# Gated delta rule on one core: triangular inverse in blocks of 16 joined to 32, other numbers between the steps, final norm in column halves

## The chip, the cores and the metric

The kernel runs on one core of a Trainium2 chip. The metric is device time in microseconds (us). The kernel before took 1869.27 us as the median of 3 runs (1867.79 to 1872.93).

## What is computed

The kernel computes one decoder layer for a prompt of 1024 columns (tokens) and for 8 samples of 4 columns, with the same weights: a projection `w_in`, two branches on parts of it (a gated delta rule and an HGRN2 recurrence), their projections, a gate, `w_out`, an FFN with a short convolution, and a final RMSNorm. The change touches the triangular solve of the delta rule and the final norm. Of the reference this matters:

```python
# _gated_delta: chunks of CHUNK_A = 64, 4 heads, key and value width 128
lmat = jnp.where(strict, jnp.einsum('nbhid,nbhjd->nbhij', kb, k) * decay, 0.0)
a_mat = eye + lmat
T = lax.linalg.triangular_solve(a_mat, jnp.broadcast_to(eye, a_mat.shape), left_side=True, lower=True)
value = jnp.einsum('nbhij,nbhje->nbhie', T, v * beta[..., None])
...
# per chunk, in sequence
u = value_n - jnp.einsum('bhcd,bhde->bhce', kcd_n, S)
o = jnp.einsum('bhcd,bhde->bhce', qg_n, S) + jnp.einsum('bhij,bhje->bhie', attn_n, u)
S = S * jnp.exp(gl_n)[..., None, None] + jnp.einsum('bhcd,bhce->bhde', kg_n, u)
...
# _rmsnorm, used at the end on the prompt and on the samples
y = xf * lax.rsqrt(jnp.mean(xf * xf, axis=-1, keepdims=True) + EPS) * g.astype(jnp.float32)
```

## The kernel before

**Dense work.** All 1056 columns go through one dense projection after another. Each f32 operand is split into a high and a low part (`whi`, `wlo`, `hhi`, `hlo`), and `mm3` (L105 to L111) adds three products: L109, L110 and L111. A *dense block* is one step of `proj_cm`: 8 row tiles by 3 products, 24 matmuls of 128x352 into one PSUM buffer, then one eviction. PSUM has four buffers for dense blocks (`PSD`) and four for all other products (`PSM`). Weights come in pairs of column tiles (`load_w`): a DMA on SP to `wraw` (L96), a cast to `whi` on ACT (L83) and a subtraction to `wlo` on DVE (L84). A pair serves 6 dense blocks; two pairs are in flight.

**What sets the order.** The engines take their instructions in program order. The two recurrences are generators, and between their steps they yield a number n; `drive` hands it to `fill`, a queue of the dense blocks of `w_in` (132 blocks in all), which then puts n blocks into the order:

```python
def __call__(self, n):
    self.acc += n
    while self.acc >= 1.0 and self.q:
        self.acc -= 1.0
        self.step()
```

After every second step, `drive` also puts in one step of the samples' own generator. The phases are: norm and first projections; HGRN in four groups of 256 columns (`hgrn_group`); the delta rule in four groups (`gdn_group`); the store of the conv cache (L245 to L249); then the load of the branch outputs `oT_d`, whatever is left of `fill`, the split to `ohi` and `olo`, the branch projections, `w_out`, the FFN in 11 chunks, and in the last chunk of `down` the final norm (L1294 to L1298, with `norm`, L169 to L177).

**One delta group.** It holds 8 pairs of a 128-column tile and a head. Transposes of q, k, v (L689), the decay matrices (L710) and the products of k with k and q (L718) give `UA` (L719, DVE): for each pair the transposed strictly lower matrix beside the attention matrix. Then:

- four DMAs on SP put the 32x32 diagonal blocks into `dU` in DRAM (L725), four more load `Db` (L730), laid out with one block to a partition of 1024 elements;
- DVE negates `Db` (L739) and substitutes row by row: 31 steps of a product `Pt` (L744) and a sum into `X` (L746), with yields of 0.7 at rows 8, 16 and 24;
- four DMAs on SP store `X` to `dX` (L750), four load it back as `Yd` (L756), now with the rows of a block on the partitions; a yield of 3.5;
- DVE transposes `Yd` to `Xd` (L758), ACT copies `Yd` into `UA` (L762);
- PE joins blocks of 32 to 64 (L768, L776, L779) and 64 to 128 (L791 to L797) by small products, with evictions between them;
- the chunk steps follow (L812 to L830), then `head_post` (L580 to L600) with a yield of 2.2 and the transposes L597, and the store to `oT_d` (L848).

In `X`, partition 32b+j holds column j of the eight blocks number b of the pairs:

```python
for r in range(1, 32):
    w = r + 1
    nc.vector.tensor_tensor(Pt[:, :, 0:w], X[:, :, 0:w],
                            Db[:, 0:w, r:w].rearrange("p s o -> p o s").broadcast_to([P, 8, w]), ALU.mult)
    nc.vector.tensor_reduce(X[:, :, r], Pt[:, :, 0:w], axis=mybir.AxisListType.X, op=ALU.add)
```

## Time and profile before

| | before |
|---|---|
| median of 3 runs | 1869.27 us |
| profiled execution | 1866.14 us |
| span of its trace | 1864.4 us |
| PE busy | 1738.4 us, 93% |
| DVE busy | 927.8 us, 50% |
| ACT busy | 526.4 us, 28% |
| POOL busy | 187.5 us, 10% |
| mean granted TensorE clock | 0.965 |

The profile is of one execution, which took 1866.14 us by the same measure as the median; its trace spans 1864.4 us. An engine is busy while one of its instructions runs; PE can be busy at full clock (granted clock 1.0) or below it. A line such as L768 names the line of the kernel, then come the operation, `out<-in` by the program's names, and the tile's size.

### The profile page before, as it was taken

Reading aid. Unit: us, or ns where it says so; the run is one execution under the profiler, and the core shown is the slowest. Engines: PE = TensorE matmul, PEld = TensorE weight load, DVE = VectorE, ACT = ScalarE, POOL = GpSimd, SP = SyncE. Lnnn points to the kernel's source line nnn. Section 1 sums busy time; section 2 is a strip of 40 time slices with the busy share of each in tenths; the row PEclk is TensorE's granted clock in tenths of the full one; section 3 lists DMA queues with packets and bytes.
Section 4 is the critical chain, followed back from the end, with each engine's and each line's share of the span. In section 5 each row is a group of like instructions: output and inputs, shape, how many; then the busy total and the mean of one; then the engine's idle time right before and its main releaser. Section 6 shows DMA issues by size and latency. Waiting matters only on the chain.

```text
span 1864.4 us, 30256 instructions
## 1 busy us (share of the span) xinstructions
PE 1738.4 (93%) x12765; PEld 1644.4 (88%) x12765; DVE 927.8 (50%) x1585; ACT 526.4 (28%) x1140; POOL 187.5 (10%) x315
## 2 busy tenths in 40 slices
PE   7999999989989999904999999999999999999998
PEld 7999989989978889803999999899899899899896
DVE  5312356774635666453552463444444444444446
ACT  5433323434324252303110242122122122122122
POOL 2100223340102020100000010000000000000001
PEclk9999999999989999856999999999999999999999
DMA  6323243444443363123343211111111111111102
GB/s 204 104 91 114 86 126 131 121 140 140 122 120 94 98 174 120 55 62 135 107 133 95 80 46 46 46 36 56 46 37 55 46 38 53 46 39 52 46 26 106
DMA packets 198931, 161.81 MB, mean 87 GB/s; under 512 B 17982, under 2 KB 184016, under 8 KB 198777
## 3 DMA queue, kind: packets, MB, share of 16 engines
q1 hardware_dynamic: 175382, 123.92, 22.6%
q10 hardware_dynamic: 23414, 35.96, 5.4%
q8 instruction: 100, 1.64, 0.4%
q14 instruction: 35, 0.29, 0.1%
HBM read 119.57 MB, written 40.21 MB: 86 GB/s over the span
## 4 chain that ended last, share of the span: by engine, by line
PE 53%; DVE 5%; ACT 2%; DMA 1%; issue 1%; POOL 1%; SPq 0%; ACTq 0%; POOLq 0%; DVEq 0%
PE pd L109 16%; PE pd L110 16%; PE pd L111 16%; DVE Pt L744 1%; DVE X L746 1%; PE pd L121 1%; POOL rs L76 1%; DVE y L177 1%; DVE tmp L177 0%; DMA raw<-oT_d 0%; PE pd L120 0%; ACT tmp L174 0%; PE pm L812 0%; DVE mlo L84 0%; PE pd L123 0%
## 5 line engine op out<-in xcount | busy, mean ns | idle before, releaser
L109 PE MATMUL pd<-hhi,whi 128*128 128x352 f32 x1056 | 351.3, 333 | 0.0
L110 PE MATMUL pd<-hlo,whi 128*128 128x352 f32 x1056 | 346.5, 328 | 0.0
L111 PE MATMUL pd<-hhi,wlo 128*128 128x352 f32 x1056 | 346.2, 328 | 0.0
L109 PE MATMUL pd<-mhi,whi 128*128 128x352 f32 x1056 | 340.5, 323 | 0.0
L110 PE MATMUL pd<-mlo,whi 128*128 128x352 f32 x1056 | 338.6, 321 | 0.6 <-DVE mlo L84 0.6
L111 PE MATMUL pd<-mhi,wlo 128*128 128x352 f32 x1056 | 338.4, 321 | 0.0
L84 DVE TENSOR_TENSOR wlo<-wraw,whi 128x1024 fp32r<-128x1024 f32 x126 | 153.3, 1227 | 198.0 <-ACT whi L83 197.5
L83 ACT CAST whi<-wraw 128x1024 fp32r<-128x1024 f32 x126 | 130.5, 1049 | 399.1 <-PE pd L111 201.9
L109 PEld LDWEIGHTS pd<-hhi,whi 128*128 128x128 f32 x1056 | 201.1, 190 | 2.2 <-issue 0.8
L110 PEld LDWEIGHTS pd<-hlo,whi 128*128 128x128 f32 x1056 | 201.4, 191 | 1.3 <-issue 0.4
L111 PEld LDWEIGHTS pd<-hhi,wlo 128*128 128x128 f32 x1056 | 201.0, 190 | 1.3 <-issue 0.6
L110 PEld LDWEIGHTS pd<-mlo,whi 128*128 128x128 f32 x1056 | 198.4, 188 | 1.3 <-DVE mlo L84 0.9
L109 PEld LDWEIGHTS pd<-mhi,whi 128*128 128x128 f32 x1056 | 198.1, 188 | 0.4
L111 PEld LDWEIGHTS pd<-mhi,wlo 128*128 128x128 f32 x1056 | 198.1, 188 | 0.0
L1289 DVE TENSOR_TENSOR x<-x,pd 128x512 f32<-128x512 f32 x176 | 118.8, 685 | 78.0 <-PE pd L111 77.6
L109 PE MATMUL pd<-whi,act 128*128 128x512 f32 x352 | 137.9, 392 | 0.1
L110 PE MATMUL pd<-wlo,act 128*128 128x512 f32 x352 | 137.2, 390 | 0.0
L111 PE MATMUL pd<-whi,act 128*128 128x512 f32 x352 | 137.0, 389 | 0.0
L218 ACT COPY z<-pd 128x352 f32<-128x352 f32 (+1 forms) x102 | 44.3, 441 | 143.7 <-PE pd L111 136.5
L1266 DVE TENSOR_TENSOR ga<-pd,ga 128x352 f32<-128x352 f32 x66 | 34.5, 522 | 98.3 <-PE pd L111 98.3
L109 PEld LDWEIGHTS pd<-whi,act 128*128 128x128 f32 x352 | 66.1, 188 | 16.2 <-PE pd L111 2.0
L109 PE MATMUL pd<-ohi,whi 128*128 128x352 f32 x192 | 62.6, 327 | 18.0 <-ACT ohi L83 18.0
(407 smaller groups left out, 2687.7 us busy)
## 6 DMA issues: line engine op xcount, KB each, us to landing
wraw<-in_w_in SPq DMA_DIRECT2D x48, 512.0 KB, 5.4
wraw<-in_w_ffn_gate SPq DMA_DIRECT2D x22, 512.0 KB, 5.0
wraw<-in_w_ffn_up SPq DMA_DIRECT2D x22, 512.0 KB, 3.7
wraw<-in_w_ffn_down SPq DMA_DIRECT2D x22, 512.0 KB, 4.0
sg_d<-sg ACTq DMA_DIRECT2D x16, 528.0 KB, 2.6
qkv_d<-sl ACTq DMA_DIRECT2D x12, 512.0 KB, 3.1
sga<-sg_d SPq DMA_DIRECT2D x12, 352.0 KB, 4.3
sgb<-sg_d SPq DMA_DIRECT2D x12, 352.0 KB, 3.0
```

The source lines that it names most:

```text
L76: nc.gpsimd.tensor_tensor(out, in_, pexp[:n, which, :w], ALU.pow)
L83: nc.scalar.copy(out=hi, in_=src)
L84: (eng or nc.vector).tensor_tensor(lo, src, hi.bitcast(F32), ALU.subtract)
L109: nc.tensor.matmul(ps, whi[:, kw], xhi[:, kx], start=q == 0, stop=False)
L110: nc.tensor.matmul(ps, whi[:, kw], xlo[:, kx], start=False, stop=False)
L111: nc.tensor.matmul(ps, wlo[:, kw], xhi[:, kx], start=False, stop=q == n - 1)
L121: nc.tensor.matmul(ps[:NS], st[:, kx, 0:NS], wlo[:, kw], start=False, stop=False)
L177: nc.vector.scalar_tensor_tensor(xn[:n], xt[:n], rs[:n], g_bc[:n], ALU.mult, ALU.mult)
L218: nc.scalar.copy(out=z[:, pad + a:pad + e], in_=ps[:, :e - a])
L744: nc.vector.tensor_tensor(Pt[:, :, 0:w], X[:, :, 0:w], Db[:, 0:w, r:w].rearrange("p s o -> p o s").broadcast_to([P, 8, w]), ALU.mult)
L1266: nc.vector.tensor_tensor(a[:, bs], ps, a[:, bs], ALU.mult)
L1289: nc.vector.tensor_tensor(x1[:, t, qs], x1[:, t, qs], ps, ALU.add)
```

## The change

The substitution runs on diagonal blocks of 16 instead of 32. Two blocks of 16 are joined to one of 32 on PE: 32 products of 32x16 from `UA` and `Xd` (L773), an eviction with the sign turned to `W5` (L774), 32 products of 32x16 from `W5` and `Yd` (L781), an addition into `Yd` (L782), a second transpose to `Xd` (L783). The old join of 32 to 64 follows as it was (L788, L794 and on). `dU` and `Yd` go in eight DMAs each of half the size, issued by SP and ACT in turn; `Db`, `X` and `Pt` shrink, and they have tiles of their own in place of shared ones. The numbers yielded fall: in a delta group 2.2 to 0.6 at the start of group 0, three yields of 0.7 in the substitution to one, 3.5 to 2.4 ahead of the transpose; two yields of 0.5 are new; `head_post` yields 2.0 for 2.2, an HGRN level 0.75 for 0.9. The 132 blocks stay 132: what isn't put between the steps comes after them. The final norm takes the squares of each half of 512 columns apart (`final_sq`), each as soon as the half is there, and multiplies and stores in halves (`final_out`), one row tile later.

```diff
-        yield 2.2
+        yield 2.0
...
-        yield 0.6 if g else 2.2
+        yield 0.6
...
         for b in range(4):
-            nc.sync.dma_start(out=dU[g, b:32:4].rearrange("c j i -> j c i"),
-                              in_=UA[32 * b:32 * b + 32, :, 0, 32 * b:32 * b + 32])
-
-        Db = os_tile([P, 32, 32], "Db")
+            for k in range(2):
+                r0 = 32 * b + 16 * k
+                (nc.sync, nc.scalar)[k].dma_start(out=dU[g, k, b:32:4].rearrange("c j i -> j c i"),
+                                                  in_=UA[r0:r0 + 16, :, 0, r0:r0 + 16])
+
+        Db = mp.tile([P, 16, 16], F32, name="Db", bufs=1)
         for b in range(4):
-            nc.sync.dma_start(out=Db[32 * b:32 * b + 32], in_=dU[g])
+            nc.sync.dma_start(out=Db[32 * b:32 * b + 32], in_=dU[g, b // 2])
...
+        nc.gpsimd.memset(Yd, 0.0)
...
-        for r in range(1, 32):
+        for r in range(1, 16):
...
         for b in range(4):
             nc.sync.dma_start(out=dX[g, :, 8 * b:8 * b + 8, :], in_=X[32 * b:32 * b + 32])
...
         for b in range(4):
-            nc.sync.dma_start(out=Yd[32 * b:32 * b + 32], in_=dX[g, b:32:4].rearrange("c s r -> s c r"))
-        yield 3.5
+            for k in range(2):
+                r0 = 32 * b + 16 * k
+                (nc.sync, nc.scalar)[k].dma_start(out=Yd[r0:r0 + 16, :, 16 * k:16 * k + 16],
+                                                  in_=dX[g, b:32:4, 16 * k:16 * k + 16].rearrange("c s r -> s c r"))
+        nc.gpsimd.memset(W5[:, :, 16:32], 0.0)
+        yield 2.4
+
         nc.vector.transpose(Xd, Yd)
+        pw = PSM()
+        pwv = pw[:, :128].rearrange("p (c s) -> p c s", s=16)
+        for p in range(8):
+            for b in range(4):
+                bs = slice(32 * b, 32 * b + 32)
+                nc.tensor.matmul(pwv[bs, p, :], UA[bs, p, 0, bs], Xd[bs, p, 0:16], start=True, stop=True)
+        nc.vector.tensor_scalar(W5[:, :, 0:16], pwv, -1.0, None, op0=ALU.mult)
+        yield 0.5
...
+                nc.tensor.matmul(pxv[bs, p, :], W5[bs, p, :], Yd[bs, p, 16:32], start=True, stop=True)
+        nc.vector.tensor_tensor(Yd[:, :, 16:32], pxv, Yd[:, :, 16:32], ALU.add)
+        nc.vector.transpose(Xd, Yd)
+        yield 0.5
...
-            yield 0.9
+            yield 0.75
...
+                if ch == NCH - 1:
+                    final_sq(t, q)
+                    if q == 0 and t != NC:
+                        final_out(t - 1 if t else NC)
...
+    def final_sq(t, q):
...
+        nc.scalar.activation(last["sq"][:n, t % NC, qs], x1t(t)[:n, qs], AF.Square, scale=D ** -0.5,
+                             accum_out=fsum[t][:n, q:q + 1])
...
+        nc.vector.scalar_tensor_tensor(rs[:n], ss[:n, 0:1], EPS, ss[:n, 1:2], ALU.add, ALU.add)
+        power(rs[:n], rs[:n], 0)
...
+        for q in range(2):
+            qs = slice(q * 512, (q + 1) * 512)
+            nc.vector.scalar_tensor_tensor(yt[:n, qs], x1t(t)[:n, qs], rs[:n], last["g"][:n, qs], ALU.mult, ALU.mult)
+            (nc.sync, nc.scalar)[q].dma_start(out=dst[:, qs], in_=yt[:n, qs])
```

What that makes of the order is shown at three places. First PE in the last delta group, from its last `L718` (`x_7752` is that group's q and k) to the first join of `Xd`; L109, L110 and L111 are the dense matmuls. Before:

```order
L718 MATMUL pm<-x_7752 128x256 x3
L710 MATMUL pm<-eem,A 128x128 x2
L109 MATMUL pd<-hhi,whi 128x352
L110 MATMUL pd<-hlo,whi 128x352
L111 MATMUL pd<-hhi,wlo 128x352
L718 MATMUL pm<-x_7752 128x256
L768 MATMUL pm<-Xd,UA 32x32 x16
```

Now, at the joins:

```order
L109 MATMUL pd<-hhi,whi 128x352
L110 MATMUL pd<-hlo,whi 128x352
L773 MATMUL pm<-Xd,UA 32x16 x32
L111 MATMUL pd<-hhi,wlo 128x352
L109 MATMUL pd<-hhi,whi 128x352
L110 MATMUL pd<-hlo,whi 128x352
L781 MATMUL pm<-Yd,W_7930 32x16 x32
L111 MATMUL pd<-hhi,wlo 128x352
```

Before, no dense matmul stood between the last L718 and L768 there; now 157 stand between the last L718 and L773, 3 between L773 and L781, and 6 between L781 and L794.

Second, ACT in delta group 0, around the DMAs of `Yd` that it issues (L540 and L542 are evictions of dense blocks, L83 is a weight cast). Before, with the evictions L564 of the gates at that place and the copies of `Yd` (L762) behind them:

```order
L564 ACTIVATE sg<-pd 128x352 x2
L83 CAST whi<-wraw 128x8x128
L564 ACTIVATE sg<-pd 128x352
L83 CAST whi<-wraw 128x8x128
L565 DMA sg_d_92<-sg 128x1056
L564 ACTIVATE sg<-pd 128x352 x2
L762 COPY UA<-Yd 32x8x32 x4
```

Now:

```order
L540 ACTIVATE sl<-pd 128x352 x2
L83 CAST whi<-wraw 128x8x128
L762 DMA Yd<-dX 16x8x16 x4
L540 ACTIVATE sl<-pd 128x320
L542 ACTIVATE og_s<-pd 128x32
L83 CAST whi<-wraw 128x8x128
L548 DMA og_d_88<-sl 128x1024
```

Four issues of `Yd` now stand on ACT between a weight cast and an eviction; the number L762 is, in the changed kernel, the line of these DMAs.

Third, PE at the end of the delta rule, from the last chunk step over the transposes of `head_post` (L597) and those of the conv cache (L245) to the first branch projection (`ohi`). Before:

```order
L828 MATMUL pm<-ut,kvt 128x128 x4
L830 MATMUL pm<-ut,UA 128x128 x4
L597 MATMUL pm<-ident,o_sb 128x128 x8
L245 MATMUL pm<-ident,cout 27x128 x12
L109 MATMUL pd<-ohi,whi 128x352 x2
```

Now:

```order
L597 MATMUL pm<-ident,o_sb 128x128 x8
L109 MATMUL pd<-hhi,whi 128x352
L110 MATMUL pd<-hlo,whi 128x352
...
L245 MATMUL pm<-ident,cout 27x128 x12
L109 MATMUL pd<-hhi,whi 128x352
L110 MATMUL pd<-hlo,whi 128x352
...
L109 MATMUL pd<-ohi,whi 128x352 x2
```

24 dense matmuls now stand between L597 and L245, and 24 between L245 and the first branch projection, where none stood before.

## Rows read from the trace of the kernel before

**Rows 1.** page, part 2: busy tenths of PE in 40 slices of 46.6 us

```profile
PE   7999999989989999904999999999999999999998
```

**Rows 2.** waits of PE: what for; us in total, times, longest us

```profile
PE pm L768 <- DVE Xd L758: 52.6, 4, 42.4
```

**Rows 3.** stretches: length, each engine busy (x instructions), granted clock, DMA share, GB/s

```profile
176.00:448.00 272.00, 257.80 (x3266) 245.07 (x3265) 166.94 (x227) 94.89 (x247) 79.33 (x90) 0.99 0.40 125
524.00:548.00 24.00, 20.17 (x217) 15.93 (x217) 3.92 (x8) 2.66 (x6) 1.08 (x3) 0.64 0.36 102
628.00:644.00 16.00, 12.82 (x143) 10.93 (x142) 5.46 (x9) 3.22 (x7) 0.78 (x2) 0.79 0.54 150
736.00:760.00 24.00, 20.86 (x179) 18.44 (x179) 5.07 (x13) 4.21 (x11) 1.08 (x3) 0.64 0.27 74
791.00:833.40 42.40, 0.00 (x1) 0.01 (x1) 26.51 (x71) 4.48 (x8) 2.72 (x7) 0.55 0.26 68
833.40:846.00 12.60, 10.45 (x132) 9.80 (x133) 4.61 (x11) 0.40 (x2) 0.78 (x2) 0.50 0.01 1
846.00:864.00 18.00, 10.56 (x76) 9.73 (x76) 7.53 (x19) 5.93 (x25) 1.64 (x1) 0.88 0.05 15
864.00:884.40 20.40, 2.42 (x10) 1.46 (x8) 5.05 (x9) 7.30 (x15) 0.00 (x0) 0.50 0.74 271
900.00:920.00 20.00, 20.00 (x128) 20.00 (x127) 12.40 (x18) 4.25 (x5) 0.00 (x0) 1.00 0.47 134
```

**Rows 4.** timeline of the last group: start, us, instruction, idle before

```profile
791.07 1.65 DVE L719 SCALAR_TENSOR_TENSOR UA<-pm,pr,EE 128x256 f32<-128x256 f32 x4
...
796.27 1.72 SPq L730 DMA_DIRECT2D Db<-dU  x4
...
802.08 0.69 DVE L739 TENSOR_SCALAR Db<-Db 128x1024 f32<-128x1024 f32 x1 [6.74 <-DMA Db<-dU]
...
811.03 0.38 DVE L744 TENSOR_TENSOR Pt<-X,Db 128x128 f32<-128x128 f32 x1
...
826.55 1.72 SPq L750 DMA_DIRECT2D dX<-X  x4
...
829.58 1.80 SPq L756 DMA_DIRECT2D Yd<-dX  x4
...
832.90 0.45 DVE L758 STREAM_TRANSPOSE Xd<-Yd 128x256 f32<-128x256 f32 x1 [6.44 <-DMA Yd<-dX]
...
833.40 1.06 PE L768 MATMUL pm<-Xd,UA 32*32 32x32 f32 x32 [42.41 <-DVE Xd L758]
```

**Rows 5.** timeline of DVE in group 2

```profile
704.30 0.18 DVE L744 TENSOR_TENSOR Pt<-X,Db 128x16 f32<-128x16 f32 x1 [0.31 <-POOL Db L740]
...
710.08 1.23 DVE L84 TENSOR_TENSOR wlo<-wraw,whi 128x1024 fp32r<-128x1024 f32 x1 [3.17 <-ACT whi L83]
...
733.33 0.42 DVE L746 TENSOR_REDUCE X<-Pt 128x8 f32<-128x256 f32 x1
...
740.54 0.45 DVE L758 STREAM_TRANSPOSE Xd<-Yd 128x256 f32<-128x256 f32 x1 [4.52 <-DMA Yd<-dX]
```

**Rows 6.** timeline of ACT in group 0: a weight cast and an eviction

```profile
514.32 1.05 ACT L83 CAST whi<-wraw 128x1024 fp32r<-128x1024 f32 x1 [3.19 <-PE pd L110]
515.27 0.46 ACT L564 ACTIVATE sg<-pd 128x352 f32<-128x352 f32 x1
```

**Rows 7.** timeline of PE at the end of the delta rule

```profile
861.12 1.97 PE L597 MATMUL pm<-ident,o_sb 128*128 128x128 f32 x8 [5.37 <-DVE o_sb L590]
862.88 2.77 PE L245 MATMUL pm<-ident,cout 128*27 128x128 f32 x12
```

**Rows 8.** timeline of PE at an HGRN level

```profile
182.92 0.70 PE L971 MATMUL pm<-qf,kk 128*32 128x16 f32 x62 [0.16 <-DVE qf L943]
```

**Rows 9.** DMA issues: size of each, median us to landing

```profile
dU<-UA SPq DMA_DIRECT2D x16, 32.0 KB, 2.3
```

**Rows 10.** timeline of ACT at the end of the kernel

```profile
1857.08 1.06 ACT L174 ACTIVATE sq<-x 128x1024 f32<-128x1024 f32 x1 [1.52 <-POOL rs L76]
```

More of the change, by code (lines that the diff above doesn't have):

```diff
@@ L750, in gdn_group @@
             nc.sync.dma_start(out=dX[g, :, 8 * b:8 * b + 8, :], in_=X[32 * b:32 * b + 32])
[L751 to L754 removed]
         for b in range(4):
[L756 to L758 removed]
+            for k in range(2):
[4 more added lines that the diff above has]
+        yield 2.4
+        nc.vector.transpose(Xd, Yd)
+        pw = PSM()
[6 more added lines that the diff above has]
+        yield 0.5
+        px = PSM()
+        pxv = px[:, :128].rearrange("p (c r) -> p c r", r=16)
+        for p in range(8):
+            for b in range(4):
+                bs = slice(32 * b, 32 * b + 32)
+                nc.tensor.matmul(pxv[bs, p, :], W5[bs, p, :], Yd[bs, p, 16:32], start=True, stop=True)
+        nc.vector.tensor_tensor(Yd[:, :, 16:32], pxv, Yd[:, :, 16:32], ALU.add)
+        nc.vector.transpose(Xd, Yd)
+        yield 0.5
         Yf = UA[:, :, 0, :]
@@ L1293, in down, with final_out @@
                         nc.vector.tensor_tensor(x1s[:, qs], x1s[:, qs], ps[r * NS:(r + 1) * NS], ALU.add)
-            if ch == NCH - 1:
-                yt = last["y"][:, t, :D] if t < NC else gp.tile([P, T], F32, name="yts", tag="sl")[:, :D]
-                norm(t, x1t(t), last["g"], const, yt, last["sq"][:, t % NC, :D])
-                dst = y_p.rearrange("b s d -> (b s) d")[t * P:(t + 1) * P, :] if t < NC else \
-                    y_s.rearrange("b s d -> (b s) d")
-                nc.sync.dma_start(out=dst, in_=yt[:n])
+                if ch == NCH - 1:
+                    final_sq(t, q)
+                    if q == 0 and t != NC:
+                        final_out(t - 1 if t else NC)
+        if ch == NCH - 1:
+            final_out(NC - 1)
+    fsum = {}
+    def final_sq(t, q):
+        n = rows(t)
+        if q == 0:
+            fsum[t] = const.tile([P, 2], F32, name="fss", bufs=3)
+        qs = slice(q * 512, (q + 1) * 512)
+        nc.scalar.activation(last["sq"][:n, t % NC, qs], x1t(t)[:n, qs], AF.Square, scale=D ** -0.5,
+                             accum_out=fsum[t][:n, q:q + 1])
+    def final_out(t):
+        n = rows(t)
+        ss = fsum[t]
+        rs = const.tile([P, 1], F32, name="frs", bufs=3)
+        nc.vector.scalar_tensor_tensor(rs[:n], ss[:n, 0:1], EPS, ss[:n, 1:2], ALU.add, ALU.add)
+        power(rs[:n], rs[:n], 0)
+        yt = last["y"][:, t, :D] if t < NC else gp.tile([P, T], F32, name="yts", tag="sl")[:, :D]
+        dst = y_p.rearrange("b s d -> (b s) d")[t * P:(t + 1) * P, :] if t < NC else y_s.rearrange("b s d -> (b s) d")
+        for q in range(2):
+            qs = slice(q * 512, (q + 1) * 512)
+            nc.vector.scalar_tensor_tensor(yt[:n, qs], x1t(t)[:n, qs], rs[:n], last["g"][:n, qs], ALU.mult, ALU.mult)
+            (nc.sync, nc.scalar)[q].dma_start(out=dst[:, qs], in_=yt[:n, qs])
     gate_up(0)
```

21 lines of the change are left out of this document (11 added, 10 removed).

## The prediction

> **What bounds the kernel now.** I read the 40 slices first [rows 1]: PE is busy nine tenths of nearly every slice, so the time is PE's work plus the stretches in which PE stands or runs at half clock. Two slices stand out, the 18th and 19th (from 792 us to 886): busy 0 and 4 tenths. The list of waits names the cause [rows 2]: the join of the delta rule (L768) waited for the transposed substitution result Xd four times, 52.6 us in all, 42.4 us of it once, in the last group, where no dense matmul is left to run. Then I priced the stretches as length minus busy time times granted clock [rows 3]. In an undisturbed stretch (900 to 920) PE starts 128 dense matmuls in 20.00 us: 0.156 us each, 3.75 us for a dense block of 24.
> - Groups 0 to 2: 24 - 20.17*0.64 = 11.1, 16 - 12.82*0.79 = 5.9 and 24 - 20.86*0.64 = 10.6: 27.6 us lost. The waits at L768 are only 10.2 of that (52.6 - 42.4); the other 17.4 are the clock at its lower level, 1.2 GHz, after each of the three holes, 5.8 us a hole.
> - Last group, 791 to 884.4 (93.4 us): the full-clock work in it is 0 + 10.45*0.50 + 10.56*0.88 + 2.42*0.50 = 15.7 us, so 77.7 us are lost.
>
> These 105 us are what the change can reach. The chain behind L768 is in rows 4: the last UA ends at 792.7, dU is stored, Db loaded (L739 starts at 802.08), 31 steps run on DVE until 826.5, dX and Yd go through DRAM, Xd, and L768 at 833.40: 40.7 us with nothing else running. With dense work running it is longer, since DVE is used in order: in group 2 the steps take 29.4 us (704.30 to 733.75), with one stop for a weight split that itself waited 3.17 us for ACT [rows 5]. Ahead of L768 in groups 0 to 2 PE's order holds 281 to 291 dense matmuls, 44 to 45 us: just too little.
>
> **The change, part by part.**
> *Steps.* 15 instead of 31. From L739 (802.08) to the end of the step of width 16 (811.03 + 0.38 and a reduction of about 0.3) is 9.7 us, against 24.4 to the dX store at 826.55; L739 itself works on a quarter of the elements, at most 0.35 less. Saved: 15.1 us of chain.
> *Transfers.* dU and Yd become eight DMAs each, four on SP and four on ACT at the same time, so SP's issue time stays. Db carries 128 instead of 512 KB: from its first issue (796.27) to L739 are 5.8 us now; the nearest small transfer, Yd, takes 3.3 from 829.58 to 832.90 [rows 4]. Between 3.3 and 5.8 I take 3.5, saving 2.3, since it is now nearly as small as Yd. dX and Yd (826.55 to 832.90) keep their 6.35 us. The new chain is 40.7 - 15.1 - 2.3 = 23.3 us. All pieces of dU halve from 128 to 64 bytes; today's land in 2.3 us [rows 9]. The Trainium skill (DMA: Bandwidth & Descriptors, Specifications) says that writes under 512 B cost a read-modify-write. Today's pieces are already under that size and the trace shows no more than the 2.3 us; what the rule would make of 64 bytes stands with the first rival below.
> *Cover.* With fewer yields the order puts 161, 163, 161 and 157 dense matmuls between the last L718 and the first join (L773) of groups 0 to 3: 25.1, 25.4, 25.1 and 24.5 us. UA ends some 0.75 us after the last L718, so 23.7 to 24.7 us count against 23.3 of chain.
> *ACT's queue.* Half of Yd is now issued by ACT. In group 0 these four issues (0.45 us each, like L756's) stand behind a weight cast that waits until PE has finished a dense block; behind them stand that block's eviction, the second cast, and on DVE two weight splits ahead of the transpose. From the end of that block this takes 1.05 (cast) + 4*0.45 + 0.46 (eviction) + 1.05 + 1.23 (split) + 0.45 (transpose) plus hand-overs, about 6.4 us [rows 4 to 6], and PE has 38 dense matmuls, 5.9 us, to bridge it; if the chain arrives later, a hole of 1 to 1.5 us. Group 1 is alike (0.5 to 1). In groups 2 and 3 the transpose stands ahead of the splits: about nothing. PE has four PSUM buffers for dense blocks, so a late eviction stops nobody. These holes sum to 2 to 3 us; I add one that grows by 2 and brings a clock fall (5.8), since the margins are under 1 us: 10 us for the four groups. Bounds: 0, and the first rival.
> *Last group.* Its dense cover hides the chunk work of 15.7 us too. What stays is the way from the last transposes (L597, 861.12) over the conv cache (L245) and the loads of the branch outputs to the first projection, 884.4: 23.3 us [rows 3, 7]. The order now has 48 dense matmuls in it (7.5 us), but L245 stands behind the first 24, which makes the way about 1 us longer. L597 and L245 took 1.97 + 2.77 us at half clock, 2.4 at full. Left: 24.3 - 7.5 - 2.4 = 14.4 us (10 if the loads start earlier, 20 if the fall of the clock outlasts them).
> *Added PE work.* 64 small matmuls a group. L768 shows as 32 rows for its 16 instructions, so 128 rows a group, 512 in all. The nearest rows: L971 goes through four column groups in turn, 0.70 us for 62, 11 ns each [rows 8]; L768 uses two, 1.06 us for 32, 33 ns [rows 4]. The new ones use four, so I take 11 ns, 6 us; upper bound 17 us. The Trainium skill (TensorE: Matmul & The Clock Gate, section "Wait — 56ns, not 53.3ns?") gives about 25 ns from start to start at the least; by that it would be 12.8 us and the sum 7 us higher, within the range. L971's row does not bear it out for matmuls on separate column groups.
> *New waits.* L781 waits for one eviction behind L773, L794 for an add and a transpose (0.45 us like L758) behind L781. 3 and 6 dense matmuls stand there (0.47 and 0.94 us): about 0.25 us each stays, 2 us over the groups.
> *HGRN and start.* With 0.75 for 0.9 and 2.0 for 2.2, six levels of groups 1 to 3 stand closer together. That stretch idles 14.2 us over 28 levels, 0.5 each [rows 3]; between 0 and three times that for each of the six is 0 to 9, I take 3, and 1 for the first delta group, whose loads (0.6 for 2.2) have less ahead of them.
> *Final norm.* After the last matmul come one Square of 1.06 us [rows 10], a power and a product over the whole width. The Square halves, and the first half of the product is stored during the second: 1 us gained (0 to 2). DVE stays as busy, two products of half the width.
>
> **Sum.** The profiled execution took 1866.1 us (span 1864.4). Last group -(77.7 - 14.4) = -63.3; holes of groups 0 to 2 -(27.6 - 10) = -17.6; PE work +6; new waits +2; HGRN and start +4; norm -1: together -70, 1796 us. The median of the runs is 3.1 above that execution: 1799.
>
> **Rivals.**
> *1. The hole is shared out, not removed.* The cover falls from 44 to 25 us in three groups. If the chain with company is 5.5 us longer than I think, as group 2's steps were (29.4 against 23.7 from the end of L739 to 826.5) [rows 4, 5], each group has a hole of 5.5 us and a fall of 5.8: 45 instead of 10, 1834 us. For it: weight splits still stand ahead of L747 in groups 1 to 3, and margins are under 1 us. Against it: the stop in rows 5 came from a split in the midst of the steps, and the new order has none there. The rule of the Trainium skill on pieces under 512 B (DMA: Bandwidth & Descriptors, Specifications) would act here: as an estimate by it, doubling the 2.3 us of the two transfers in 64-byte pieces adds 4.6 us to each chain, near the 5.5 of this rival; 2.3 us for 128-byte pieces [rows 9] speak against it.
> *2. Slower than before.* The same mechanism at its limit: the chain keeps its old length while the cover is cut. The place is L773 of each group; its four waits plus falls must eat 10 + 70 us, 20 each, a hole of 14.2, a chain of 38.6 us. In group 2 the way from the first step to Xd takes 36.7 us (704.30 to 740.99), in the last group 30.6 (802.77 to 833.35), so its chain has some 47 [rows 4, 5]; at that length it would be 4*(22.5 + 5.8) = 113, 1902 us. For it only the eight more DMA issues on ACT, each behind work that waits for PE; against it rows 4, where the removed steps are seen on the chain.
> *3. Better.* No fall and no hole in the four groups (-10), an end of 10 (-4), nothing lost in HGRN (-4): 1781.
> That the dense work still runs out before the last group is excluded: the order has 157 dense matmuls in it.
>
> **Chances.** Forecast (1787 to 1815) 0.59; rival 1 (1815 to 1850) 0.22; rival 3 (1775 to 1787) 0.12; rival 2 0.05; within 0.3% (about what a measurement of this kernel can tell from no change, 5.6 us) 0.02. The range 1779 to 1832 takes in both bounds of the added PE work and leaves out the upper part of rival 1 (0.09), rival 2, the case of no change and 0.04 below. Faster 0.93, same 0.02, slower 0.05.
>
> **What would show it.** Right: slices 18 and 19 of the new profile busy 7 tenths or more; the wait of L773 for Xd under 8 us over four waits; the dU-to-Xd chain of each group at 23 to 26 us; one stretch of 12 to 18 us without PE work ahead of the first projection, after L245; L773 and L781 with under 0.02 us a row. Wrong: waits at L773 of 4 us or more in several groups with the clock at 1.2 GHz behind them; casts on ACT that hold Yd; more than 10 us of new idle time in the HGRN groups.

## The result

The changed kernel takes 1809.83 us (median of 4 runs, 1804.39 to 1810.65) against 1869.32 before (4 runs, 1867.79 to 1872.93): a ratio of 0.9673, 95% interval 0.9649 to 0.9697. The forecast was 1799, the range 1779 to 1832. So the time lies in the range, 11 us above the forecast. The profiled execution took 1809.22 us with a span of 1807.5: 56.9 us less span, where the sum of the prediction had 70.

### The profile page after: what moved, and what is told of

Same layout as the page of the kernel before. It is cut to its first block, busy times and chain, and to the rows that moved or that the text cites. A ratio compares the mean times of both kernels' runs of the same rounds, so it can differ in the third digit from the quotient of the medians.

```text
span 1807.5 us, 31280 instructions
## 1 busy us (share of the span) xinstructions
PE 1730.7 (96%) x13277; PEld 1637.3 (91%) x13277; DVE 877.2 (49%) x1478; ACT 529.1 (29%) x1158; POOL 183.0 (10%) x323
## 4 chain that ended last, share of the span: by engine, by line
PE 55%; DVE 4%; DMA 2%; ACT 1%; issue 1%; POOL 1%; SPq 0%; ACTq 0%; DVEq 0%; POOLq 0%
PE pd L109 17%; PE pd L110 17%; PE pd L111 17%; PE pd L121 1%; DVE y L1348 1%; DMA raw<-oT_d 1%; DVE Pt L752 0%; DVE tmp L177 0%; PE pd L120 0%; ACT tmp L174 0%; DVE X L754 0%; POOL rs L76 0%; DVE mlo L84 0%; PE pd L123 0%; DMA Yd<-dX 0%
## 5 line engine op out<-in xcount | busy, mean ns | idle before, releaser
L109 PE MATMUL pd<-hhi,whi 128*128 128x352 f32 x1056 | 350.7, 332 | 0.0
L111 PE MATMUL pd<-hhi,wlo 128*128 128x352 f32 x1056 | 345.7, 327 | 0.0
L110 PE MATMUL pd<-hlo,whi 128*128 128x352 f32 x1056 | 344.6, 326 | 0.0
L109 PE MATMUL pd<-mhi,whi 128*128 128x352 f32 x1056 | 340.5, 323 | 0.0
L110 PE MATMUL pd<-mlo,whi 128*128 128x352 f32 x1056 | 338.6, 321 | 0.6 <-DVE mlo L84 0.6
L111 PE MATMUL pd<-mhi,wlo 128*128 128x352 f32 x1056 | 338.3, 321 | 0.0
L83 ACT CAST whi<-wraw 128x1024 fp32r<-128x1024 f32 x126 | 130.4, 1049 | 399.4 <-PE pd L111 202.0
L109 PEld LDWEIGHTS pd<-hhi,whi 128*128 128x128 f32 x1056 | 200.3, 190 | 2.0 <-issue 0.6
L110 PEld LDWEIGHTS pd<-hlo,whi 128*128 128x128 f32 x1056 | 200.6, 190 | 0.8
L111 PEld LDWEIGHTS pd<-hhi,wlo 128*128 128x128 f32 x1056 | 200.4, 190 | 0.8
L110 PEld LDWEIGHTS pd<-mlo,whi 128*128 128x128 f32 x1056 | 198.4, 188 | 1.3 <-DVE mlo L84 0.9
L109 PEld LDWEIGHTS pd<-mhi,whi 128*128 128x128 f32 x1056 | 198.0, 188 | 0.4
L111 PEld LDWEIGHTS pd<-mhi,wlo 128*128 128x128 f32 x1056 | 198.0, 188 | 0.0
L109 PE MATMUL pd<-whi,act 128*128 128x512 f32 x352 | 138.1, 392 | 0.1
L110 PE MATMUL pd<-wlo,act 128*128 128x512 f32 x352 | 137.2, 390 | 0.0
L111 PE MATMUL pd<-whi,act 128*128 128x512 f32 x352 | 137.0, 389 | 0.0
L109 PEld LDWEIGHTS pd<-whi,act 128*128 128x128 f32 x352 | 66.1, 188 | 16.2 <-PE pd L111 1.6
L109 PE MATMUL pd<-ohi,whi 128*128 128x352 f32 x192 | 62.8, 328 | 18.3 <-ACT ohi L83 18.3
```

The costliest lines, as they stand in the source:

```text
L83: nc.scalar.copy(out=hi, in_=src)
L109: nc.tensor.matmul(ps, whi[:, kw], xhi[:, kx], start=q == 0, stop=False)
L110: nc.tensor.matmul(ps, whi[:, kw], xlo[:, kx], start=False, stop=False)
L111: nc.tensor.matmul(ps, wlo[:, kw], xhi[:, kx], start=False, stop=q == n - 1)
```

## The profile after

First the same part of the page that [rows 1] showed, the busy tenths of PE in 40 slices (now of 45.2 us), and below it the granted clock:

```profile
PE   7999899989999989987999999999999999999997
PEclk9999999999999899998999999999999999999999
```

The slices of 0 and 4 tenths are gone: the 18th and 19th now have 8 and 7 (the forecast was 7 or more). The lowest, the 19th, is 813 to 859 us. The list of waits of PE (what for; us in total, times, longest), to hold against [rows 2]:

```profile
PE pd L109 <- ACT ohi L83: 18.3, 1, 18.3
...
PE pm L773 <- DVE Xd L767: 2.4, 3, 1.0
...
PE pm L794 <- issue: 2.2, 1, 2.2
```

The wait for Xd fell from 52.6 us to 2.4. What leads now is the wait of the first branch projection (`ohi`), and there is a new wait, in L794, for which the profile names nothing that was late. The first of the two is not new. It stood behind the other in the list of before, as long as now:

```profile
PE pd L109 <- ACT ohi L83: 18.0, 1, 18.0
```

For an account by stretch I cut both traces at the first transpose of each delta group (L689) and at the first branch projection. These are the rows by stretch (length; busy time and instructions of PE, PEld, DVE, ACT, POOL; granted clock; DMA share; GB/s): first of the kernel before, the HGRN stretch and the four delta groups,

```profile
176.00:448.90 272.90, 258.70 (x3272) 245.95 (x3271) 166.94 (x227) 95.78 (x248) 79.33 (x90) 0.99 0.40 124
448.90:564.80 115.90, 108.32 (x826) 99.50 (x825) 55.28 (x144) 40.55 (x108) 13.23 (x16) 0.93 0.40 119
564.80:664.80 100.00, 94.55 (x684) 89.99 (x682) 57.42 (x143) 37.10 (x106) 10.98 (x17) 0.97 0.37 111
664.80:774.20 109.40, 103.63 (x705) 97.85 (x704) 61.69 (x145) 38.51 (x105) 14.11 (x18) 0.92 0.40 120
774.20:883.60 109.40, 38.45 (x311) 33.99 (x309) 53.30 (x136) 26.67 (x83) 8.67 (x12) 0.66 0.25 82
```

then of the kernel after:

```profile
176.00:446.10 270.10, 250.51 (x3225) 238.17 (x3224) 165.34 (x227) 94.94 (x246) 74.66 (x90) 0.99 0.41 124
446.10:534.10 88.00, 83.73 (x785) 76.97 (x784) 39.98 (x114) 37.04 (x100) 9.94 (x16) 1.00 0.38 117
534.10:629.80 95.70, 92.02 (x813) 85.84 (x812) 44.63 (x113) 33.62 (x97) 13.32 (x19) 0.93 0.35 106
629.80:720.20 90.40, 83.45 (x732) 77.92 (x730) 46.80 (x114) 37.66 (x106) 16.08 (x20) 0.98 0.44 129
720.20:825.60 105.40, 85.52 (x755) 80.61 (x753) 45.13 (x110) 36.01 (x100) 7.97 (x7) 0.91 0.36 117
```

Idle time is length less PE's busy time. The dense matmuls of `w_in` in each stretch are counted in the trace and priced at 0.156 us. "Half clock" is half of PE's busy time that lies at 1.2 GHz, and what is left is other PE work, the small products mostly:

| stretch | idle before, after | half clock before, after | dense before, after | other before, after |
|---|---|---|---|---|
| HGRN | 14.2, 19.6 | 3.4, 3.4 | 1194, 1147 | 68.7, 67.8 |
| group 0 | 7.6, 4.3 | 8.3, 0.0 | 443, 339 | 30.8, 30.8 |
| group 1 | 5.4, 3.7 | 3.4, 6.8 | 420, 357 | 25.6, 29.4 |
| group 2 | 5.8, 7.0 | 8.3, 1.7 | 440, 339 | 26.6, 28.8 |
| group 3 and end | 71.0, 19.9 | 7.7, 1.7 | 41, 357 | 24.3, 28.0 |

Without the dense work, the four groups took 224.7 us before and 162.0 after: idle time -54.9, half clock -17.5, other work +9.7. HGRN took 4.5 us more. From the first branch projection to the span's end both kernels need the same within 1.1 us.

The chain of the last group, the same instructions as in [rows 4] (start, us, engine, instruction, idle time before):

```profile
736.88 1.66 DVE L719 SCALAR_TENSOR_TENSOR UA<-pm,pr,EE 128x256 f32<-128x256 f32 x4
...
745.87 0.29 DVE L747 TENSOR_SCALAR Db<-Db 128x256 f32<-128x256 f32 x1 [1.41 <-DMA Db<-dU]
...
754.82 0.29 DVE L754 TENSOR_REDUCE X<-Pt 128x8 f32<-128x128 f32 x1
...
758.49 1.74 SPq L762 DMA_DIRECT2D Yd<-dX  x4
...
762.43 0.45 DVE L767 STREAM_TRANSPOSE Xd<-Yd 128x256 f32<-128x256 f32 x1 [7.33 <-DMA Yd<-dX]
...
762.93 0.73 PE L773 MATMUL pm<-Xd,UA 32*32 32x16 f32 x64 [0.96 <-DVE Xd L767]
```

From the end of UA (738.5) to L773 it takes 24.4 us instead of 40.7, and PE is idle for 0.96 of it.

## Experiments

The times of the changed kernels are medians of 4 runs; before was run on the same chip each time.

| kernel | us | before, same chip |
|---|---|---|
| old steps, new numbers | 1855.38 | 1867.66 |
| new steps, old numbers | 1814.86 | 1867.66 |
| changed, again | 1809.29 | 1867.66 |
| changed, conv store early | 1798.97 | 1867.66 |
| changed, stream shifted | 1813.74 | 1870.86 |
| changed, joins of 16 twice | 1837.78 | 1870.86 |
| changed, transfers on SP alone | 1817.15 | 1870.86 |
| early store, column blocks | 1791.90 | 1870.86 |
| the same, again | 1794.88 | 1871.29 |
| the same, fewer products | 1801.28 | 1871.29 |
| changed, branch weights on ACT | 1806.12 | 1870.66 |

**Which half carries the gain.** Two kernels, each with one half of the change. The first keeps the 31 steps:

```diff
-        yield 2.2
+        yield 2.0
...
-        yield 0.6 if g else 2.2
+        yield 0.6
...
-            if r % 8 == 0:
+            if r == 8:
...
-        yield 3.5
+        yield 2.4
         nc.vector.transpose(Xd, Yd)
+        fill(1.0)
...
-            yield 0.9
+            yield 0.75
```

> The kernel before with the new numbers alone (2.0, 0.6, 0.75, one 0.7 instead of three, 2.4, and 1.0 behind the transpose); 31 steps and the old transfers stay. Its order has 285, 298, 290 and 28 dense matmuls ahead of the four joins (before: 281, 291, 285, 0), so the numbers hardly change the cover of groups 0 to 2. Theory A (the shorter chain is what frees dense work for the last group): 28 dense matmuls hide 4.4 us of the last hole, the HGRN stretch loses about 4.6 as in the changed kernel, so 1865 to 1873 us, and the wait of the join for Xd in the last group is still 36 to 40 us. Rival B (sharing out the cover with the numbers is the gain): 1840 or less, with waits of about 15 us in every group. Rival C (sharing alone hurts, as in the second rival of the prediction): 1890 or more.

It took 1855.38, 12.3 us less than before. Rivals B and C fall, but so does the size that I gave for A. The wait for Xd (its line is L769 there):

```profile
PE pm L769 <- DVE Xd L758: 44.2, 4, 39.7
```

The last group still waits 39.7 us, as A had it. But the other three waits sum to 4.5 us, where they were 10.2, and in groups 1 and 2 the clock stays at full (half clock 0.0 by the account above, where it was 3.4 and 8.3). A few more dense matmuls ahead of a join (4 to 7) fill part of a hole that was 3 to 4 us long, and in two groups the fall of the clock behind it goes too.

The second half has the new steps with the old numbers, the changed kernel with

```diff
-        yield 2.0
+        yield 2.2
...
-        yield 0.6
+        yield 0.6 if g else 2.2
...
-        yield 2.4
+        yield 3.9
...
-            yield 0.75
+            yield 0.9
```

> The changed kernel with the numbers of before (2.2, 0.6 or 2.2, 0.9; 3.9 in place of 2.4, so that with the two new 0.5 the sum behind UA grows by 1.5). Its order has 179, 172, 163 and 152 dense matmuls ahead of the four joins of 16, but none behind the last of them: the chunk steps of the last group and the end stretch have no cover. Theory A: the four waits stay near 2 to 4 us in total, the HGRN stretch gets back about 5 us of idle time, the last group loses about 10 to 15 in its chunk steps and at the end, so 1810 to 1822 us: the numbers are worth under 12 us, the steps over 45. Rival B (the numbers carry the gain): 1840 or more.

1814.86, within theory A's range: the steps alone are worth 52.8 us, the numbers alone 12.3, both together 58.4. The last group shows what the numbers do. With the old ones all dense work is used up ahead of its first join, and its idle time is 33.9 us instead of 19.9; but HGRN idles 14.7 us instead of 19.6.

**The end of the delta rule.** In the changed kernel the way from L597 to the first branch projection takes 28.3 us (797.35 to 825.65), where it was 22.5 (861.12 to 883.62). The 48 dense matmuls that now stand there hid none of the 18 us of idle time: the way grew with them. What the timeline shows of it, PE first, then ACT and SP:

```profile
797.35 1.04 PE L597 MATMUL pm<-ident,o_sb 128*128 128x128 f32 x8
802.04 1.47 PE L245 MATMUL pm<-ident,cout 128*27 128x128 f32 x12
...
825.65 0.96 PE L109 MATMUL pd<-ohi,whi 128*128 128x352 f32 x2 [18.29 <-ACT ohi L83]
```

```profile
799.42 0.38 ACTq L874 DMA_DIRECT2D oT_d<-og  x1
...
807.59 0.31 ACTq L249 DMA_DIRECT2D out<-rowt  x1
...
809.57 0.37 SPq L96 DMA_DIRECT2D wraw<-in_w_branch_a  x1
809.99 0.56 SPq L96 DMA_DIRECT2D wraw<-in_w_branch_b  x1
...
811.56 1.51 SPq L1172 DMA_DIRECT2D raw<-oT_d  x3
```

The branch outputs are stored at 799.42, but their load (`raw`) is issued at 811.56, 12.1 us later. Before, the same load came 7.2 us after that store (863.91), also behind the store of the conv cache:

```profile
871.10 1.52 SPq L1146 DMA_DIRECT2D raw<-oT_d  x3
```

Three kernels ask what held it. The first moves the conv cache's store:

```diff
     for g in range(NG):
+        if g == NG - 1:
+            store_conv_cache(cout, 12, 27, cq_p[0, 0], cq_s.rearrange("l b t c -> (l b t) c"), mp, "z")
         St = drive(gdn_group(g, St))
-    store_conv_cache(cout, 12, 27, cq_p[0, 0], cq_s.rearrange("l b t c -> (l b t) c"), mp, "z")
```

> The changed kernel with the store of the conv cache ahead of the last delta group instead of behind it. In the changed kernel L597 to the first branch projection takes 28.35 us, of which 18.3 idle: the loads of the branch outputs start at 811.56, 12 us after the store to oT_d was issued (799.42), behind the conv cache's last store (807.6) and two weight loads on SP. Theory A (the loads wait for that store, since their buffer takes the space of the tiles it reads): the loads start 2 to 4 us after the store to oT_d, the hole falls from 18.3 to 8 to 13 us, and the time falls by 6 to 10, to 1800 to 1804. Rival D (the loads are set by the transfer of 4.2 MB, or by something else that is late): under 2 us of change.

1798.97, 10.3 us less than the changed kernel on the same chip. The load is issued at 803.04, 4 us after the store to oT_d, and the hole is 12.9 us. That is theory A, at the upper end of its ranges or just past it, but in this kernel's order the two weight loads on SP also stand behind the load. So a second kernel took them off SP and left the store late:

```diff
-    def load_w(parts, eng=None):
+    def load_w(parts, eng=None, queue=None):
...
-                nc.sync.dma_start(out=raw[:, k0:k0 + nk, :w], in_=ap.rearrange("(k p) n -> p k n", p=P))
+                (queue or nc.sync).dma_start(out=raw[:, k0:k0 + nk, :w], in_=ap.rearrange("(k p) n -> p k n", p=P))
...
-            hi, lo = load_w([[(H, wba[:, d * P:(d + 1) * P]), (H, wbb[:, d * P:(d + 1) * P])] for d in (d0, d0 + 1)])
+            hi, lo = load_w([[(H, wba[:, d * P:(d + 1) * P]), (H, wbb[:, d * P:(d + 1) * P])] for d in (d0, d0 + 1)], queue=nc.scalar)
```

> The changed kernel with the weight loads of the branch projections issued by ACT instead of SP; the store of the conv cache stays late. In the changed kernel the chain of waits runs from the split of a branch weight (L84, until 809.55) to two weight loads on SP (809.57 to 810.55), and only then to the loads of the branch outputs (811.56). The early store of the conv cache had also moved these weight loads behind the others on SP, so that run does not tell the two apart. Theory P (the weight loads on SP hold them): the first load of the branch outputs is issued 3 to 5 us after the store to oT_d (799.42 in the changed kernel), the hole shrinks by 5 to 9 us, 1799 to 1805 us. Theory A (the conv cache's last store holds them, through the space of its tiles): it is issued 1 to 2 us behind that store's last issue (807.59), some 10 us after the store to oT_d, the hole shrinks by 1 to 3, 1806 to 1810.

1806.12, and the load is issued at 811.15. The store to oT_d stands here in ACT's timeline:

```profile
800.74 0.37 ACTq L874 DMA_DIRECT2D oT_d<-og  x1
```

The chain of waits (start, us, what) runs over the conv cache's store and its landing:

```profile
808.69 0.25 ACTq L248
...
808.98 1.52 DMA out<-rowt
...
811.15 0.56 SPq L1172
```

So it is the store in the main: the buffers of `raw` take the space of the tiles that it reads. From the issue of L248 to the landing took 1.8 us, by which that store was done at 809.1 in the changed kernel, and the weight loads held SP until 810.55. Counted from the store to oT_d, the load of `raw` starts after 10.4 us here, 12.1 in the changed kernel and 4.0 with the early store, so the weight loads add 1.7 us to what the store holds back. Taking away the loads alone leaves the store, and the hole stays at 18.5 us.

The third kernel has the early store, and the loads of `raw` by the column blocks in which they are used:

```diff
-    for x, a, b in ((1, 0, T), (0, 0, last), (0, last, T)):
-        if a:
+    for x, a, b in ((1, 0, BW), (0, 0, BW), (1, BW, 2 * BW), (0, BW, 2 * BW), (1, 2 * BW, T), (0, 2 * BW, last),
+                    (0, last, T)):
+        if a == last:
```

> The kernel with the early store of the conv cache, and with the loads of the branch outputs cut by the column blocks of 352 in which they are used, the first block of both branches first (1.4 MB instead of 3.6 MB ahead of the first split). There the first split starts 9.2 us after the first of these loads is issued (803.04 to 812.26). Theory L (it waits for the bytes): it starts 4 to 6 us after the issue, the hole ahead of the first branch projection shrinks by 3 to 5 us, 1794 to 1796. Rival M (the fixed time of a transfer, or the last dense work, holds it): under 1.5 us.

```profile
800.88 8.84 SPq L1174 DMA_DIRECT2D raw<-oT_d  x7
...
805.63 1.64 ACT L83 CAST ohi<-raw 128x352 fp32r<-128x352 f32 x4 [0.61 <-DMA raw<-oT_d]
...
807.99 0.95 PE L109 MATMUL pd<-ohi,whi 128*128 128x352 f32 x2 [5.19 <-ACT ohi L83]
```

Theory L, and more than it had: the first split starts 4.75 us after the first load, and the hole is 5.2 us (7.4 in the second round of runs), down from 12.9. With 1791.90 and 1794.88 us in two rounds of runs (ratios 0.9584, 0.9555 to 0.9614, and 0.9593, 0.9577 to 0.9609) this kernel is the fastest here, 14 to 18 us below the changed one.

**The stop in L794.** In the trace of the changed kernel PE runs 24 of the 32 rows of L794 in group 1, stands for 2.19 us, and runs the other 8. No engine and no transfer that L794 needs is late. The page's part 3 (queue, kind: packets, MB, share) has a line for the fetch of PE's instructions, and the rows by stretch show how much PE ran between three of these packets, which start at 546.8, 566.4 and 587.2:

```profile
q8 instruction: 104, 1.70, 0.4%
```

```profile
546.80:566.40 19.60, 18.51 (x125) 17.06 (x124) 11.59 (x23) 9.05 (x13) 7.12 (x6) 1.00 0.38 106
566.40:587.20 20.80, 20.80 (x257) 20.08 (x257) 11.51 (x37) 5.11 (x12) 0.91 (x6) 1.00 0.40 119
```

104 packets of 16 KB feed 26,554 rows of PE and PEld (a row is one instruction in the trace; the page's 13,277, twice), 255 a packet; the kernel before has 100 for 25,530 rows. Between most packets PE runs 200 to 340; between the last two it is 514, counted to the stop itself 542 since the packet of 566.4 began. PE goes on 1.5 us after the next packet has landed (587.2, 1.2 us long). The products of L773 and L781 run 128 rows each, weight loads counted, within 0.7 us; as many in dense work take 10 us. Theory F is that PE used up its instructions faster than they came. The changed kernel, run again, was to show whether the stop is chance:

> The changed kernel unchanged, for comparisons on the same chip: 1804 to 1811 us. Its first profile has one stop of 2.19 us within the products of L794 in group 1, for which nothing in the profile is late, with a fall of the clock behind it (6.8 us of clock loss). If it is set by the program (its small products in a row), it comes again at the same place, within 1 us of the same length; if it is chance, it is absent or elsewhere, and the time is 5 to 9 us lower without it.

1809.29 us, and the stop is there again, 2.23 us in L794 of group 1, with 5.1 us of half clock. It is set by the program, not by chance. Then 32 products ahead of the first group that nothing reads, to shift the fetch:

```diff
+    shift = PSM("shift")
+    for i in range(32):
+        nc.tensor.matmul(shift[0:32, 16 * i:16 * i + 16], ident[0:32, 0:32], ident[0:32, 0:16], start=True, stop=True)
     St = None
```

> The changed kernel with 32 products of 32x16 from the identity (64 rows of PE, 128 with their weight loads; nothing reads them) ahead of the first delta group. In both profiles of the changed kernel PE stops for 2.2 us within L794 of group 1; the trace shows 104 packets of 16 KB on the instruction queue, one for about 255 rows of PE, and there PE had run 513 rows since the packet before and went on 1.4 us after the next had landed. Theory F (PE ran out of instructions, since small products use them up faster than they are fetched): 128 rows more shift the place at which the fetch is due, the stop in group 1 goes or shrinks below 1 us, and the time falls by 5 to 9 us from 1809, unless another group gets one. Rival G (the stop is bound to that place, by the transfers of weights and vx that fill the DMA queues there at 583 to 588): it stays at 2 us and so does the time, 1808 to 1812.

1813.74 us. Neither expectation was met: the stop in L794 is gone, but there are two others, 1.66 us behind the small products L802 and L805 of group 1 and 1.23 in those of group 2. The stop moved, which speaks against G, and the time did not fall. The next kernel runs each loop of 32 products twice:

```diff
-        for p in range(8):
+        for p in 2 * list(range(8)):
             for b in range(4):
                 bs = slice(32 * b, 32 * b + 32)
                 nc.tensor.matmul(pwv[bs, p, :], UA[bs, p, 0, bs], Xd[bs, p, 0:16], start=True, stop=True)
...
-        for p in range(8):
+        for p in 2 * list(range(8)):
             for b in range(4):
                 bs = slice(32 * b, 32 * b + 32)
                 nc.tensor.matmul(pxv[bs, p, :], W5[bs, p, :], Yd[bs, p, 16:32], start=True, stop=True)
```

> The changed kernel with each loop of 32 products at L773 and at L781 run twice, the second time with the same result: 512 more rows of PE in all. Theory H (they cost what they run, 11 ns a row as in the prediction): 5.7 us more of PE time, 1813 to 1817 us. Theory F (they also use up the instruction stream, 256 more rows of PE with the weight loads in a group): stops of 1 to 3 us with nothing late in the profile in two or more groups, each with a fall of the clock, and 1822 us or more. Rival I (a product costs 33 ns, the upper bound of the prediction): 17 us more, without such stops.

1837.78 us, 28 more. Its waits of PE:

```profile
PE pm L781 <- issue: 8.1, 4, 3.8
...
PE pd L109 <- issue: 4.1, 1, 4.1
```

Every group has a stop now, 2.3, 3.8, 4.1 and 1.9 us long, with 28.6 us of half clock over the four groups instead of 10.2. Counted in the trace as above, PE had run 542, 548, 546 and 547 rows since a packet began when it stopped. In the changed kernel it was 542, in its second run 548, with the stream shifted 544 and 546. That is theory F: always at nearly the same number of rows. The other traces agree: such stops are in ten of them, 15 in all, and each comes at 542 to 548 rows. The kernel with the new steps and the old numbers has the same products in another order; there at most 424 rows lie between two packets, and it has no such stop. Why a packet starts so late is not shown. One more wait without a cause in the profile, of about 2 us at the start of HGRN (L967; L941 before), is in every kernel, at some 420 rows, and this count does not explain it. 5.7 us of running time, or 17, would not give 28.

If so, fewer rows should remove the stop. With the early store and the column blocks, the 32 products of L773 became 8:

```diff
+    bd32 = mp.tile([P, P], F32, name="bd32", bufs=1)
+    nc.gpsimd.memset(bd32, 0.0)
+    for b in range(4):
+        nc.gpsimd.memset(bd32[32 * b:32 * b + 32, 32 * b:32 * b + 32], 1.0)
...
+        UD = os_tile([P, 8, P], "UD")
+        nc.gpsimd.tensor_tensor(UD, UA[:, :, 0, :], bd32.rearrange("p (o i) -> p o i", o=1).broadcast_to([P, 8, P]), ALU.mult)
...
         for p in range(8):
-            for b in range(4):
-                bs = slice(32 * b, 32 * b + 32)
-                nc.tensor.matmul(pwv[bs, p, :], UA[bs, p, 0, bs], Xd[bs, p, 0:16], start=True, stop=True)
+            nc.tensor.matmul(pwv[:, p, :], UD[:, p, :], Xd[:, p, 0:16], start=True, stop=True)
```

> The kernel with the early store and the column blocks; in it the 32 products of 32x16 at the first join of 16 become 8 of 128x16 with a copy of UA in which all but the diagonal blocks of 32 is zero (one multiplication on POOL, 128x1024, while POOL waits anyway). That is 32 rows of PE a group, weight loads counted, instead of 128. In the kernel without this PE stops 2.17 us in L794 of group 1, 512 rows after the last packet of its instruction queue. Theory F (PE runs out of instructions there): with 96 rows fewer ahead of it the stop goes, 2.2 us and 3 to 5 us of clock loss with it; 16 rows at 128 columns cost 0.2 to 1.2 us more than 64 small ones, 1 to 5 us over the groups: 1784 to 1791 us against 1792. Rival G (the stop belongs to the transfers that run there): it stays, and the time is 1792 to 1798.

The kernel without this edit, beside it on the same chip:

> The kernel with the early store and the column blocks, unchanged, for comparison with the one with fewer products on the same chip: 1787 to 1796 us, and the stop in L794 of group 1 at 2.0 to 2.3 us again.

It kept its stop (1.94 us) and took 1794.88. With fewer products the stop is gone, no more than about 370 rows lie between two packets there, and group 1 has no half clock. And yet it took 1801.28, 6.4 us more, outside the ranges of both theories. Part of that is the products: the four loops take 7.6 us instead of 2.9. The rest is the clock, in another place. By stretches of group 0, first with fewer products, then without the edit:

```profile
504.00:508.00 4.00, 3.44 (x84) 3.17 (x83) 0.74 (x2) 0.00 (x0) 0.00 (x0) 0.89 0.90 274
508.00:520.00 12.00, 12.00 (x152) 9.68 (x145) 3.53 (x8) 2.07 (x5) 1.25 (x4) 0.50 0.33 106
```

```profile
504.00:508.00 4.00, 3.25 (x140) 2.69 (x139) 1.40 (x3) 1.17 (x2) 0.00 (x0) 1.00 1.05 340
508.00:520.00 12.00, 12.00 (x193) 10.33 (x188) 4.21 (x9) 2.67 (x6) 1.55 (x5) 1.00 0.56 183
```

PE stands 0.56 us in the first row and 0.75 in the third, and still the clock falls to 1.2 GHz in the kernel with fewer products: for 1.93 us ahead of the fall PE ran L778, 16 rows of 16 columns. That these products bring the fall on is not shown; it is one place in one trace. The profiled executions of the two differ by only 0.5 us (1796.8 and 1796.3), so these traces hold no more than a part of the 6.4 us; what the other runs lost stays open.

**The split over two queues.**

```diff
-                (nc.sync, nc.scalar)[k].dma_start(out=dU[g, k, b:32:4].rearrange("c j i -> j c i"),
+                nc.sync.dma_start(out=dU[g, k, b:32:4].rearrange("c j i -> j c i"),
...
-                (nc.sync, nc.scalar)[k].dma_start(out=Yd[r0:r0 + 16, :, 16 * k:16 * k + 16],
+                nc.sync.dma_start(out=Yd[r0:r0 + 16, :, 16 * k:16 * k + 16],
```

> The changed kernel with all 16 transfers of dU and Yd of a group issued by SP. Theory J (the split over SP and ACT saves issue time): four more issues of 0.45 us for each, so the way from UA to Xd grows from 24.4 to 26.1 by 2 to 3.5 us; the order has 170, 185, 175 and 176 dense matmuls ahead of the joins (161 to 163, 157 in the changed kernel), which covers it, so the waits for Xd stay under 4 us in total, and the time changes by -2 to +4 us from 1809. Rival K (the issues on ACT were held by casts and evictions there, as the prediction had it for group 0): the way gets shorter or stays, and the time falls.

1817.15 us, but from 1805 to 1823 in four runs, so its sign is not settled. From UA to Xd the groups take 25.0, 28.9, 30.2 and 27.4 us, against 25.6, 24.6, 26.1 and 24.4 in the changed kernel. So three groups are 3.0 to 4.3 us longer, as J has it or a little more, and K falls for them; group 0 is 0.6 shorter (0.2 than in the second trace of the changed kernel), too little to say what the issues on ACT cost there. The one wait for Xd is 2.8 us, in group 2. The profiled run (1819.84 us) has two stops of the kind above, 2.5 and 1.4 us, where the changed kernel has one, and 20.1 us of half clock in the four groups instead of 10.2; that this is what goes beyond J's 4 us is read from the rows, not shown by a run.

**The final norm.** In the changed kernel, DVE at the end, and then the same in a kernel that calls `final_out` without the delay of one tile:

```diff
-                    if q == 0 and t != NC:
-                        final_out(t - 1 if t else NC)
-        if ch == NCH - 1:
-            final_out(NC - 1)
+                    if q == 1:
+                        final_out(t)
```

> The changed kernel with final_out called for a row tile right behind its second final_sq, not one tile later. In the changed kernel the last addition of L1315 begins at 1800.15 and the last product ends at 1804.60, 4.45 us, against 4.16 before the change (1856.32 to 1860.48): on DVE the two products of the tile before stand ahead of the last L1342. Theory N (that place in DVE's order eats the gain of the halves): from the start of the last addition to the end of the last product 3.6 to 3.9 us. Rival O (a halved product saves nothing in itself): 4.2 us or more. The time moves by under 1 us either way, 1804 to 1811.

```profile
1800.15 0.68 DVE L1315 TENSOR_TENSOR x<-x,pd 128x512 f32<-128x512 f32 x1
...
1800.97 1.42 DVE L1348 SCALAR_TENSOR_TENSOR y<-x,frs,g_bc 128x512 f32<-128x512 f32 x2
...
1802.30 0.15 DVE L1342 SCALAR_TENSOR_TENSOR frs<-fss 128x1 f32<-128x1 f32 x1
...
1803.18 1.42 DVE L1348 SCALAR_TENSOR_TENSOR y<-x,frs,g_bc 128x512 f32<-128x512 f32 x2 [0.73 <-POOL frs L76]
```

```profile
1797.78 0.68 DVE L1315 TENSOR_TENSOR x<-x,pd 128x512 f32<-128x512 f32 x1
1798.59 1.42 DVE L1346 SCALAR_TENSOR_TENSOR y<-x,frs,g_bc 128x512 f32<-128x512 f32 x2
1799.92 0.15 DVE L1340 SCALAR_TENSOR_TENSOR frs<-fss 128x1 f32<-128x1 f32 x1
1800.80 1.41 DVE L1346 SCALAR_TENSOR_TENSOR y<-x,frs,g_bc 128x512 f32<-128x512 f32 x2 [0.73 <-POOL frs L76]
```

4.43 us from the last addition to the last product, as against 4.45, and 1806.86 us in the one run that was made: the edit did not do what it should. The two products of the tile before still stand ahead of the last sum on DVE, so it does not tell N from O. That this place costs the gain is read from the rows and not shown by a run.

## Why the prediction was right, and where it was off

**The main term held.** The chain was said to shrink to 23.3 us in the last group and measured 24.4 (24.4 to 26.1 over the groups; forecast 23 to 26). Its parts: from the start of L747 to the last sum 9.2 us (9.35 forecast: 9.7 less 0.35); from UA to L747 7.3 instead of 9.4, 2.0 saved (2.3 forecast); from X to Xd 7.8, 1 us more than before, where no change was forecast. The waits for Xd were 2.4 us over three (under 8 over four forecast). The last group's idle time and half clock fell by 57.1 us (78.7 to 21.6), with 63.3 forecast; groups 0 to 2 by 15.3 (38.8 to 23.5), with 17.6 forecast.

**The reason for the cover was wrong.** The prediction put the 161 to 157 dense matmuls ahead of L773 down to the smaller numbers, and its second rival cut the cover while the chain stays long. The two half changes show otherwise: with the old chain and the new numbers the order puts 285, 298 and 290 there, with the new chain and the old numbers 179, 172, 163 and 152. In all four kernels the order gave each join about the work that its chain takes while dense work lasted, and the short chain is what leaves some for the last group. With that chain, the numbers decide how much stands in HGRN (1147 or 1195) and how much behind the last L597 (48 or none). The counts were right, since they came from the order.

**The end stretch was the term most off:** 14.4 us forecast, 18.3 of idle time and 1.7 of half clock measured. The way was 22.5 us before (to 883.62); the prediction took 23.3, to the end of its stretch at 884.4. The step that failed is "L245 stands behind the first 24, which makes the way about 1 us longer". The way grew by 5.8 us, not 1: L245 started 4.7 us after L597 instead of 1.8, its store is what the loads of `raw` mostly wait for, the weight loads on SP now stand ahead of them too, and from the first of these loads to the projection it took 14.1 us instead of 12.5. The early store gives 10.3 us back, more than the whole miss of this term.

**Added PE work:** the groups of L773 and L781, 256 rows each,

```profile
L773 PE MATMUL pm<-Xd,UA 32*32 32x16 f32 x256 | 2.9, 180 | 2.4 <-DVE Xd L767 2.4
...
L781 PE MATMUL pm<-Yd,W 32*32 32x16 f32 x256 | 2.9, 180 | 0.0
```

5.8 us busy, 11 ns a row, as L971 had it (6 forecast). The Trainium skill (TensorE: Matmul & The Clock Gate, section "Wait — 56ns, not 53.3ns?") gives about 25 ns from start to start at the least; these rows, spread over four column groups, do not bear that out. What the prediction had no term for is the stop that such products bring, 2.2 us and 5 to 7 of half clock in group 1. The account's +9.7 of other work is 3.9 more than these products. The likely reason is that halving overstates the clock's share before: the kernel with the old steps and the new numbers has none of these products, its groups 1 and 2 ran at full clock, and their other work is 28.9 and 28.8 us by the same account, where it was 25.6 and 26.6.

**The fall of the clock:** the prediction allowed one more for all four groups, at 5.8 us. Group 1 has it (6.8), though not for the reason given.

**HGRN** lost 4.5 us against 3 + 1. **The norm** gained nothing, 0.3 us more from the last PE work to the end, where 1 us less was forecast.

**Rival 1** (1834) was not met, and its second leg found no support: as an estimate by the rule of the Trainium skill on pieces under 512 B (DMA: Bandwidth & Descriptors, Specifications), the transfers in 64-byte pieces were to take twice as long. From the DMA issues of the changed kernel, of groups 0 and 2 (size, median us to landing):

```profile
dU<-UA SPq DMA_DIRECT2D x4, 8.0 KB, 2.3
```

```profile
dU<-UA SPq DMA_DIRECT2D x4, 8.0 KB, 1.5
```

That is no more than the 2.3 of the 128-byte pieces in [rows 9], though each transfer carries a quarter of the bytes now, so the size of the pieces alone was not tested.

## What to carry to other kernels

Where an order fills the gaps of a serial chain from a limited store of independent work, shorten the chain, since the work that it no longer needs covers the next gap; undoing each half of such a change shows which one pays. When the big hole is closed, look at what then stands ahead of the next stage's loads: here a small store held their buffers, as it had before the change, and moving it and loading what is used first gave another 14 to 18 us. Count rows, not only busy time, when a stage is cut into many small matmuls; but try the other form too, since here the kernel without the stop was not the faster one.
